# First layer's table products and chunk scan of the S5 branch: issued on GpSimd instead of VectorE

## The chip, the cores and the metric

The kernel runs on one core of a Trainium2 chip. The metric is the device time of one execution in microseconds (us), given as the median of several runs. TensorE (PE), VectorE (DVE), ScalarE (ACT), GpSimd (POOL) and SyncE (SP, which issues all the DMAs here) each work through a list of instructions of their own, in the order of that list; semaphores tie the lists together.

## What is computed

The reference runs two layers of a hybrid diffusion backbone over 128 context tokens and 512 latent tokens with a model width of 1024, in float32. Each layer forms a modulated input, one large projection of it, three branches, a gated merge and an MLP. The branch that matters here is the bidirectional S5 recurrence:

```
step = exp(log_step);  lam_bar = exp(lam * step)
b_bar = ((lam_bar - 1) / lam) * b
for d, rev in ((0, False), (1, True)):
    bu = einsum('blgc,gpc->blgp', u, b_bar[d])          # (+ lam_bar * s0 at the first token)
    states = scan(x[t] = lam_bar[d] * x[t-1] + bu[t])   # complex, 32 groups x 64 states
    y += einsum('blgp,gcp->blgc', states, c[d]).real
    finals.append(last state)
y = gelu(y + d_skip * u);  y = y * sigmoid(y @ w_glu)
```

The other two branches are a windowed and a global attention with 8 query heads each; the new keys, values and final S5 states are outputs too.

## The kernel before

**Chunks.** The kernel cuts the tokens into chunks of 8 and lays them out in 84 columns (context 0 to 17, latent 18 to 83, with one spare column for an initial state at either end). Within a chunk the recurrence is a matrix: one operator takes 8 inputs to the state contribution of the chunk (built in `s5_prep`), one takes the state ahead of a chunk to its 8 outputs (`ct`, built in `s5_tables`), and one takes the chunk's inputs to its outputs (`KK`, later `mg`, also from `s5_tables`). What is left is a recurrence over the chunk columns, which `s5_states` runs in the tile `st` [128 partitions, 84 columns, 2 (re, im), 32 groups].

**Tables.** `s5_tables` makes eight pieces b of four groups each. For every piece it forms `ct` from the input `Cm` and the powers `ec` with six products, sums and differences of 128x512 elements, through its helper `tt` (line 467): two into `mm`, one into half of `ct`, twice over. `ct` goes to DRAM by a DMA of SP (line 484). GpSimd clears `Bs` (line 487), ACT fills it (488 to 490), and TensorE multiplies `Cm` and `ct` with `Bs` (lines 496 and 498) into a bank `p_pt`, which DVE and ACT empty into `KK` (501, 502). `mm`, `ct` and `Bs` have one buffer each, so a piece can overwrite `ct` only when the matmuls and the DMA of the piece before have read it. In the first layer the pieces are drawn out of the generator during the windowed attention; in the second layer they were made during the MLP of the first.

**Scan.** `s5_states` first folds pairs of columns (`pairs(2, 3)`, four blocks of columns on DVE, lines 685 and 686), then walks 31 steps of two columns with four dependent operations each (lines 702 to 705: two products with the squared operator `M`, two sums); the first eight steps carry context and latent together (128x128 elements), the other 23 the latent alone (128x64). `pairs(1, 2)` then fills the columns in between, again in four blocks: the first block reads states up to column 19, the last one the very last state. After that `fin` is taken (line 709) and the backward half is reversed (lines 712 to 716). Only then do the matmuls of line 1055 read `st` and the `ct` tables (as `tab`).

**Order.** A scheduler of the framework sets the order within each engine's list when the program is built, by its own simulated timeline. So attention, projections, tables and scan of the first layer stand mingled in each list. While the windowed attention of layer 0 runs, DVE has to subtract for every weight tile (line 127, `wlo<-raw,whi`), empty and rotate projections (742 to 744), take row maxima of the scores (951), and so on. GpSimd has little to do: it clears tiles and takes three kinds of powers (lines 270, 776, 817); DVE's line 777 waits for the power of line 776.

Of the kernel before, what the change touches and what calls it, by code (L numbers as in the profile page):

```python
# [9 lines left out]
ALU = mybir.AluOpType  # L10
# [21 lines left out]
def net(tc, I, O, depth=DEPTH, dbg=None):  # L32
    nc = tc.nc
    V, S, G, T, SY = nc.vector, nc.scalar, nc.gpsimd, nc.tensor, nc.sync
    dbg = dbg or {}

    def ap(t, off, dims):
        return bass.AP(tensor=t.tensor, offset=t.offset + off, ap=[list(d) for d in dims])
# [4 lines left out]
    def dump(name, t):  # L43
        if name in dbg:
            SY.dma_start(dbg[name], t)
# [20 lines left out]
    def ppt():  # L66
        return bank("pt", 2)
# [391 lines left out]
    def s5_tables(l, pl_, keep):  # L459

        Bb, ec, dP, delta, vw, ew = (keep[n] for n in ("Bb", "ec", "dP", "delta", "vw", "ew"))

        def pt(name, shape, bufs=1):
            return pl_.tile(shape, F32, name=name, tag=f"{name}_{l}", bufs=bufs)

        def tt(o, a, b, op):
            V.tensor_tensor(o, a, b, op=op)

        for b in range(8):
            gs = slice(4 * b, 4 * b + 4)  # L470
            s4 = slice(0, 4)
            Cm = pt("Cm", [128, 2, 4, 16], 2)
            SY.dma_start(Cm, I["ssm_c"][l, :, :, gs])
            S.activation(Cm[:, 1], Cm[:, 1], AF.Copy, scale=-1.0)
            mm, ct = (pt(n, [128, 2, 4, 8, 16]) for n in ("mm", "ct"))
            m1, m2 = mm[:, 0], mm[:, 1]

            tt(m1, vw(Cm, 0, s4), ew(ec, 0, gs), ALU.mult)
            tt(m2, vw(Cm, 1, s4), ew(ec, 1, gs), ALU.mult)
            tt(ct[:, 0], m1, m2, ALU.add)  # L480
            tt(m1, vw(Cm, 1, s4), ew(ec, 0, gs), ALU.mult)
            tt(m2, vw(Cm, 0, s4), ew(ec, 1, gs), ALU.mult)
            tt(ct[:, 1], m1, m2, ALU.subtract)
            SY.dma_start(ctab_d[l][b], ct)

            Bs = pt("Bs", [128, 2, 4, 48])
            G.memset(Bs, 0.0)
            S.activation(Bs[:, :, :, 0:16], Bb[:, :, gs], AF.Copy)
            S.activation(Bs[0:64, :, :, 16:32], Bb[0:64, :, gs], AF.Copy)
            S.activation(Bs[64:128, :, :, 32:48], Bb[64:128, :, gs], AF.Copy)  # L490
            yield
            p = ppt()
            for q in range(4):
                o = p[32 * q:32 * q + 32]
                for r_ in range(2):
                    T.matmul(o[:, 0:16], Bs[:, r_, q, 0:32], Cm[:, r_, q, :], start=(r_ == 0), stop=(r_ == 1))
                for r_ in range(2):
                    T.matmul(o[:, 16:144], Bs[:, r_, q, 16:48], ct[:, r_, q].rearrange("p t o -> p (t o)"), start=(r_ == 0), stop=(r_ == 1))
            if b % 4 == 0:
                KK = pt("KK", [128, 4, 144])  # L500
            V.scalar_tensor_tensor(KK[:, b % 4, 0:16], delta, dP[:, b:b + 1], p[:, 0:16], op0=ALU.mult, op1=ALU.add)
            S.activation(KK[:, b % 4, 16:144], p[:, 16:144], AF.Copy)
            if b % 4 == 3:

                g0 = 4 * (b - 3)
                for q in range(4):
                    o = (g0 + q) * 3840
                    SY.dma_start(ap(kk_d[l], o + 7 * 16, [[240, 16], [4 * 3840, 4], [1, 128]]), KK[32 * q:32 * q + 16, :, 0:128])
                    SY.dma_start(ap(kk_d[l], o, [[240, 16], [4 * 3840, 4], [1, 112]]), KK[32 * q + 16:32 * q + 32, :, 32:144])
                for j in range(8):  # L510
                    SY.dma_start(mg_d[l][16 * j:16 * j + 16, g0:g0 + 16], ap(kk_d[l], g0 * 3840 + (7 - j) * 16, [[240, 16], [3840, 16], [1, 128]]))
            yield


    def phase_a(l, h):
# [94 lines left out]
        def ubuf():  # L610
            return sp.tile([128, 704], F32, name="ub", tag="ub", bufs=2)

        def s5_in(b, io):

            if b % 2 == 0:
                ubs[0] = load_u(b // 2)
            ub = ubs[0]
            for r_ in range(2):
                p = psc()
                for q in range(4):  # L620
                    T.matmul(p[:, q * NCH:(q + 1) * NCH], io[:, r_, q], ub[:, (b % 2) * 4 + q], start=True, stop=True)
                v = p[:, :4 * NCH].rearrange("p (g c) -> p c g", g=4)
                S.activation(st[0:64, 1:NCH, r_, 4 * b:4 * b + 4], v[0:64, 0:NCH - 1], AF.Copy)
                for a, e in segs:
                    S.activation(st[64:128, a + 1:e, r_, 4 * b:4 * b + 4], v[64:128, e - 1:a:-1], AF.Copy)
# [32 lines left out]
        def s5_states():  # L658

            for b in range(8) if l > 0 else ():  # L660
                io = sp.tile([128, 2, 4, 128], F32, name="tab", tag="tab", bufs=TAB)
                SY.dma_start(io, inop_d[l][b])
                s5_in(b, io)
            G.memset(st[:, 0:2], 0.0)
            G.memset(st[64:128, 18], 0.0)


            L0, L1 = lam8[l][:, 0], lam8[l][:, 1]
            M = sp.tile([128, 4, 2, 32], F32, name="l16")
            V.tensor_copy(M[:, 2, 0], L0[:, 0])  # L670
            V.tensor_copy(M[:, 2, 1], L1[:, 1])
            V.tensor_tensor(M[:, 3], L1, M[:, 2, ::-1], op=ALU.mult)
            V.tensor_tensor(M[:, 2], L0, M[:, 2], op=ALU.mult)
            V.tensor_tensor(M[:, 2], M[:, 2], M[:, 3], op=ALU.add)
            V.tensor_copy(M[:, 0], M[:, 2, 0:1].to_broadcast([128, 2, 32]))
            V.tensor_scalar(M[:, 1, 0], M[:, 2, 1], -1.0, None, op0=ALU.mult)
            V.tensor_copy(M[:, 1, 1], M[:, 2, 1])

            def pairs(src, dst):

                for e, k, n in ((V, 0, 10), (V, 10, 10), (V, 20, 10), (V, 30, 11)):
                    x_, o = (st[:, c + 2 * k:c + 2 * (k + n) - 1:2] for c in (src, dst))
                    tm = ubuf()[:, 0:64 * n].rearrange("p (n a b) -> p n a b", a=2, b=32)
                    for xv, lv in ((x_, L0), (x_[:, :, ::-1], L1)):
                        e.tensor_tensor(tm, xv, lv.unsqueeze(1).to_broadcast([128, n, 2, 32]), op=ALU.mult)
                        e.tensor_tensor(o, o, tm, op=ALU.add)

            pairs(2, 3)
            SY.dma_start(st[:, 19], I["state0"][:, l])
            for s in range(31):  # L690
                a = sp.tile([128, 2, 2, 32], F32, name="sa", tag="sa", bufs=1)
                c = sp.tile([128, 2, 2, 32], F32, name="sb", tag="sb", bufs=1)
                ns = 2 if s < 8 else 1
                cur = 2 * s + (1 if ns == 2 else 19)

                def at(i):
                    return st[:, i:i + 1] if ns == 1 else st[:, i:i + 19:18]

                def lb(t):
                    return t.unsqueeze(1).to_broadcast([128, ns, 2, 32])  # L700

                V.tensor_tensor(a[:, 0:ns], at(cur), lb(M[:, 0]), op=ALU.mult)
                V.tensor_tensor(c[:, 0:ns], at(cur)[:, :, ::-1, :], lb(M[:, 1]), op=ALU.mult)
                V.tensor_tensor(a[:, 0:ns], a[:, 0:ns], at(cur + 2), op=ALU.add)
                V.tensor_tensor(at(cur + 2), a[:, 0:ns], c[:, 0:ns], op=ALU.add)
            pairs(1, 2)

            fin = sp.tile([128, 2, 2, 32], F32, name="fin", tag="sa", bufs=1)[:, 0].rearrange("p a b -> p (a b)")
            S.activation(fin, st[:, 17].rearrange("p a b -> p (a b)"), AF.Copy)

            for a, e, n in ((0, 18, 9), (18, 84, 10), (28, 74, 10), (38, 64, 10), (48, 54, 3)):
                x0, x1 = st[64:128, a:a + n], st[64:128, e - n:e]
                tm = ubuf()[64:128, 0:n * 64].rearrange("p (n a b) -> p n a b", n=n, a=2)
                S.activation(tm, x0, AF.Copy)
                V.tensor_copy(x0, x1[:, ::-1])
                S.activation(x1, tm[:, ::-1], AF.Copy)
            dump("st", st)
            return fin

        if l > 0:  # L720
            fin = s5_states()
# [131 lines left out]
        if l == 0:  # L853
            fin = s5_states()
# [185 lines left out]
        for b in range(8):  # L1040
# [9 lines left out]
            for q in range(4):  # L1050
                o = p[:, q * NCH:(q + 1) * NCH]
# [496 lines left out]
    for l in range(depth):  # L1548
        M = phase_a(l, h)
# [99 lines left out]
```

## Time and profile before

| quantity | value |
|---|---|
| median of 3 runs | 2345.88 us (2345.13 to 2347.99) |
| the profiled execution, own time | 2344.87 us |
| its span in the trace | 2343.1 us |
| PE busy | 2252.5 us (96% of the span) |
| DVE busy | 1570.4 us (67%) |
| ACT busy | 1083.2 us (46%) |
| POOL busy | 40.5 us (2%) |

Busy shares are means over the whole program. Stretches of the span are told by their start and end in us from the span's start. In the rows below, `a<-b` names the tile written and the tiles read; "idle before" is what the engine sat idle just ahead of an instruction, with the one that ended the wait. TensorE's granted clock is given as a share of full speed.

### The profile page before, as it was taken

The page shows a single profiled execution, that of the slowest core. Times are in us where ns is not written, and L with a number is a line of the kernel's source. Part 1 is how long each engine was busy: PE and PEld are TensorE (multiplying, and loading weights), DVE is VectorE, ACT ScalarE, POOL GpSimd, SP SyncE. Part 2 cuts the span into 40 slices and gives each one's busy share as a digit, 9 for nine tenths or more (in the row PEclk, how much of TensorE's full clock was granted, in tenths as well). Part 3 has the DMA queues.
Part 4 walks back from the last instruction along what each step waited for, and adds up shares of the span by engine and source line. Part 5 has one row for each costly group of instructions (what it writes and reads, how often), then busy time and mean ns, then how long its engine had stood idle before and what let it go on. Part 6 is the DMA issues. An engine that isn't in the chain of part 4 may idle for free. (4 is left out here: it accounts for less than half of the span.)

```text
span 2343.1 us, 38503 instructions
## 1 busy us (share of the span) xinstructions
PE 2252.5 (96%) x14736; PEld 2039.5 (87%) x14736; DVE 1570.4 (67%) x3471; ACT 1083.2 (46%) x2569; POOL 40.5 (2%) x75
## 2 busy tenths in 40 slices
PE   7998999999998999999999999989999989999998
PEld 4988896799997988887888998989999878999986
DVE  7789945766358955455667499357763596776688
ACT  3455554665344443222234457456652356444441
POOL 0000100000000000000000001000000000000000
PEclk9999999999999999999999999989999999999999
DMA  7423366622242345445454522552212412222231
GB/s 274 113 89 101 113 201 207 209 73 78 73 153 66 100 170 172 136 160 167 141 152 141 156 68 88 159 175 84 83 55 81 171 46 90 76 79 83 83 106 63
DMA packets 124536, 283.16 MB, mean 121 GB/s; under 512 B 37024, under 2 KB 56608, under 8 KB 124352
## 3 DMA queue, kind: packets, MB, share of 16 engines
q1 hardware_dynamic: 124352, 280.70, 37.6%
q8 instruction: 116, 1.90, 0.3%
q14 instruction: 68, 0.56, 0.1%
HBM read 243.59 MB, written 41.25 MB: 122 GB/s over the span
## 5 line engine op out<-in xcount | busy, mean ns | idle before, releaser
L126 ACT ACTIVATE whi<-raw 128x512 fp32r<-128x512 f32 x454 | 282.6, 631 | 409.4 <-PE p_g L1250 100.3
L127 DVE TENSOR_TENSOR wlo<-raw,whi 128x512 fp32r<-128x512 f32 x454 | 311.2, 690 | 228.8 <-ACT whi L126 220.8
L163 PE MATMUL p_g<-hl,whi 128*128 128x384 f32 (+1 forms) x1040 | 325.9, 314 | 5.9 <-DVE hl L127 5.9
L162 PE MATMUL p_g<-hh,whi 128*128 128x384 f32 (+1 forms) x1040 | 327.7, 316 | 0.3 <-DVE rt L743 0.3
L164 PE MATMUL p_g<-hh,wlo 128*128 128x384 f32 (+1 forms) x1040 | 325.8, 314 | 0.2
L163 PEld LDWEIGHTS p_g<-hl,whi 128*128 128x128 f32 x1040 | 199.9, 192 | 6.8 <-DVE hl L127 6.8
L162 PEld LDWEIGHTS p_g<-hh,whi 128*128 128x128 f32 x1040 | 199.6, 192 | 6.0 <-ACT rl L1422 4.2
L164 PEld LDWEIGHTS p_g<-hh,wlo 128*128 128x128 f32 x1040 | 199.3, 192 | 1.0 <-DVE wlo L127 0.9
L162 PE MATMUL p_g<-act,whi 128*128 128x384 f32 x448 | 141.8, 317 | 5.6 <-DVE mt L1120 3.4
L127 DVE TENSOR_TENSOR pl<-p_pt,ph 128x512 fp32r<-128x512 f32 (+1 forms) x176 | 103.3, 592 | 59.5 <-ACT ph L126 43.6
L163 PE MATMUL p_g<-act,whi 128*128 128x384 f32 x448 | 139.6, 312 | 0.0
L173 PE MATMUL p_g<-whi,hh 128*128 128x256 f32 x480 | 138.2, 290 | 1.2 <-DVE rt L743 0.7
L164 PE MATMUL p_g<-act,wlo 128*128 128x384 f32 x448 | 139.3, 311 | 0.0
L174 PE MATMUL p_g<-wlo,hh 128*128 128x256 f32 x480 | 137.3, 288 | 1.1 <-DVE wlo L127 1.1
L175 PE MATMUL p_g<-whi,hl 128*128 128x256 f32 x480 | 136.3, 286 | 0.0
L126 ACT ACTIVATE ph<-p_pt 128x512 fp32r<-128x512 f32 (+1 forms) x176 | 90.2, 522 | 78.4 <-PE p_pt L972 77.6
L163 PE MATMUL p_sc<-hl,whi 128*128 128x384 f32 (+1 forms) x384 | 120.0, 313 | 2.7 <-DVE hl L127 2.7
L162 PE MATMUL p_sc<-hh,whi 128*128 128x384 f32 (+1 forms) x384 | 120.8, 316 | 0.0
L164 PE MATMUL p_sc<-hh,wlo 128*128 128x256 f32 (+1 forms) x384 | 119.8, 312 | 0.0
L951 DVE TENSOR_REDUCE part<-p_sc 128x1 f32<-128x384 f32 (+2 forms) x160 | 83.4, 527 | 30.9 <-PE p_sc L941 19.4
L972 PE MATMUL p_pt<-ident,P 128*128 128x128 f32 x576 | 96.2, 278 | 7.7 <-ACT P L963 5.6
L1248 PE MATMUL p_sc<-whi,ff 128*128 128x512 f32 x248 | 98.9, 400 | 0.0
(538 smaller groups left out, 5957.4 us busy)
## 6 DMA issues: line engine op xcount, KB each, us to landing
raw<-in_w_mod_dram SPq DMA_DIRECT2D x96, 512.0 KB, 4.6
raw<-in_w_up_dram SPq DMA_DIRECT2D x64, 512.0 KB, 3.7
raw<-in_w_down_dram SPq DMA_DIRECT2D x64, 512.0 KB, 3.6
raw<-in_w_gate_dram SPq DMA_DIRECT2D x48, 512.0 KB, 3.6
raw<-in_w_br_dram SPq DMA_DIRECT2D x24, 512.0 KB, 7.4
raw<-in_w_q_dram SPq DMA_DIRECT2D x16, 512.0 KB, 3.7
ctab_d<-ct SPq DMA_DIRECT2D x16, 512.0 KB, 2.6
tab<-ctab_d SPq DMA_DIRECT2D x16, 512.0 KB
```

The lines of the kernel that those rows point to most:

```text
L126: S.activation(hi, src, AF.Copy)
L127: V.tensor_tensor(lo, src, hi, op=ALU.subtract)
L162: T.matmul(out, wh, tok(ah, t0, t1), start=(first and k == 0), stop=False)
L163: T.matmul(out, wh, tok(al, t0, t1), start=False, stop=False)
L164: T.matmul(out, wl, tok(ah, t0, t1), start=False, stop=(last and k == n - 1))
L173: T.matmul(out, ah, wh, start=(first and k == 0), stop=False)
L174: T.matmul(out, ah, wl, start=False, stop=False)
L175: T.matmul(out, al, wh, start=False, stop=(last and k == n - 1))
L951: V.reduce_max(part[:, 0, z_:z_ + 1], pp[z_][:, 0:n4], axis=AX.X, negate=True)
L972: T.transpose(p[:, (2 * (z - z0) + z_) * 128:(2 * (z - z0) + z_ + 1) * 128], Ps[z_][:, z * 128:(z + 1) * 128], ident)
L1248: T.matmul(banks[t], a_, wh, start=(k == 0), stop=False)
```

## The change

In layer 0 (`l == 0`) the helper `tt` of `s5_tables` and the four operations of each scan step are issued on GpSimd (`G`) instead of DVE (`V`). Layer 1 keeps DVE for both. The two foldings `pairs`, the making of `M`, the copies and everything else stay where they were.

```
 def tt(o, a, b, op):
-    V.tensor_tensor(o, a, b, op=op)
+    (V if l else G).tensor_tensor(o, a, b, op=op)
...
-    V.tensor_tensor(a[:, 0:ns], at(cur), lb(M[:, 0]), op=ALU.mult)
-    V.tensor_tensor(c[:, 0:ns], at(cur)[:, :, ::-1, :], lb(M[:, 1]), op=ALU.mult)
-    V.tensor_tensor(a[:, 0:ns], a[:, 0:ns], at(cur + 2), op=ALU.add)
-    V.tensor_tensor(at(cur + 2), a[:, 0:ns], c[:, 0:ns], op=ALU.add)
+    (V if l else G).tensor_tensor(a[:, 0:ns], at(cur), lb(M[:, 0]), op=ALU.mult)
+    (V if l else G).tensor_tensor(c[:, 0:ns], at(cur)[:, :, ::-1, :], lb(M[:, 1]), op=ALU.mult)
+    (V if l else G).tensor_tensor(a[:, 0:ns], a[:, 0:ns], at(cur + 2), op=ALU.add)
+    (V if l else G).tensor_tensor(at(cur + 2), a[:, 0:ns], c[:, 0:ns], op=ALU.add)
```

Since the scheduler orders the whole program anew, all lists differ for the first 400 us or so, and in places of layer 1. In the pieces below a number after a tile's name tells its buffers apart (`ct_2371` is the `ct` of table piece 3, `mm_2625` and `Bs_2634` belong to piece 4, `p_pt_2639` is the bank of piece 4).

GpSimd's list from the clearing of `st` on, before: clearings and one power, nothing else.

```order
L664 MEMSET st_717 128x128 [waits Activation_49,Pool_49]
L487 MEMSET Bs_2180 128x384 [waits PE_49]
L487 MEMSET Bs_2343 128x384 [waits PE_49,Activation_49,Pool_49]
L776 ISA
L776 TENSOR_TENSOR ksq_1642<-ksq_1642,mh_73 128x10 [waits DVE_49]
L487 MEMSET Bs_2379 128x384 [waits PE_49,Activation_49,Pool_49]
L487 MEMSET Bs_2634 128x384 [waits PE_49,Activation_49,Pool_49]
```

GpSimd's list after the change, at table piece 3, in the middle of the scan's steps with one state column (128x64):

```order
L467 TENSOR_TENSOR ct_2371<-mm_2370 128x512 [waits DMAHW2_49,PE_49]
L487 MEMSET Bs_2379 128x384
L705 TENSOR_TENSOR st_717<-sa_1936,sb_1937 128x64 [waits Pool_49]
L467 TENSOR_TENSOR mm_2370<-Cm_2367,ec_0_305 128x512 [waits Pool_49]
L467 TENSOR_TENSOR mm_2370<-Cm_2367,ec_0_305 128x512
L702 TENSOR_TENSOR sa_1942<-st_717,l16_1804 128x64 [waits Pool_49]
L703 TENSOR_TENSOR sb_1943<-st_717,l16_1804 128x64
L467 TENSOR_TENSOR ct_2371<-mm_2370 128x512 [waits Pool_49]
L704 TENSOR_TENSOR sa_1942<-sa_1942,st_717 128x64 [waits Pool_49]
L467 TENSOR_TENSOR mm_2625<-Cm_2622,ec_0_305 128x512 [waits DMAHW6_49,Pool_49]
L467 TENSOR_TENSOR mm_2625<-Cm_2622,ec_0_305 128x512 [waits Activation_49]
L705 TENSOR_TENSOR st_717<-sa_1942,sb_1943 128x64 [waits Pool_49]
```

So scan and tables now share one list, and a table operation that waits for TensorE (`PE_49`) or for a DMA holds the scan behind it. In that list, from the first operation of the scan to its last, stand 32 scan operations of 128x128, 92 of 128x64, 24 table operations of 128x512, four clearings of `Bs` and the power of line 776.

DVE's list at the end of the scan, before: the last operations of the scan, and behind them the last block of `pairs(1, 2)` (`ub_2035`, line 685) with no wait for another engine; this stands far behind table piece 4.

```order
L704 TENSOR_TENSOR sa_2014<-sa_2014,st_717 128x64 [waits DVE_49]
L705 TENSOR_TENSOR st_717<-sa_2014,sb_2015 128x64 [waits DVE_49]
L685 TENSOR_TENSOR ub_2035<-st_717,lam8_100 128x704 [waits DVE_49]
L715 COPY st_717<-st_717 64x576 [waits Activation_49]
L686 TENSOR_TENSOR st_717<-st_717,ub_2035 128x11x64 [waits DVE_49]
L987 TENSOR_TENSOR qw_1128<-p_pv_2794,yt_2887 64x256 [waits PE_49,Activation_49]
L988 TENSOR_TENSOR qw_1128<-p_pv_2794,yt_2887 64x256
L951 TENSOR_REDUCE part_3094<-p_sc_3096 128x1 [waits PE_49]
L951 TENSOR_REDUCE part_3136<-p_sc_3137 128x1 [waits PE_49]
L897 SCALAR_TENSOR_TENSOR qs_2904<-p_pt_2905,qs_2904 64x4x128 [waits Activation_49]
L898 SCALAR_TENSOR_TENSOR qs_2904<-p_pt_2905,qs_2904 64x4x128
L685 TENSOR_TENSOR ub_2035<-st_717,lam8_100 128x704 [waits DVE_49]
```

DVE's list after the change, at the same block: it now stands just ahead of the query tile `qs_2612` and of the score maxima of the third block of queries, and ahead of the matmuls of table piece 4.

```order
L987 TENSOR_TENSOR qw_1128<-p_pv_2510,yt_2595 64x256 [waits PE_49,Activation_49]
L988 TENSOR_TENSOR qw_1128<-p_pv_2510,yt_2595 64x256
L685 TENSOR_TENSOR ub_2035<-st_717,lam8_100 128x704 [waits Pool_49]
L1002 TENSOR_TENSOR qw_1128<-qw_1128,p_pt_2606 128x512 [waits DVE_49]
L897 SCALAR_TENSOR_TENSOR qs_2612<-p_pt_2613,qs_2612 64x4x128 [waits PE_49,Activation_49]
L898 SCALAR_TENSOR_TENSOR qs_2612<-p_pt_2613,qs_2612 64x4x128
L951 TENSOR_REDUCE part_2795<-p_sc_2797 128x1 [waits PE_49]
L742 TENSOR_TENSOR rt_3747<-p_g_3717,rq_1118 128x256 [waits DMAHW4_49,Activation_49]
L686 TENSOR_TENSOR st_717<-st_717,ub_2035 128x11x64 [waits DVE_49]
L743 TENSOR_TENSOR rt_3747<-p_g_3717,rq_1118 128x256
L951 TENSOR_REDUCE part_2841<-p_sc_2842 128x1 [waits PE_49]
L715 COPY st_717<-st_717 64x576 [waits Activation_49]
```

What moved: the 172 operations are gone from DVE's list, the blocks of `pairs(1, 2)` stand earlier among the attention's work, and the first operation of each of the four blocks now carries a wait for GpSimd.

## Rows read from the trace of the kernel before

**Rows 1.** Busy time, share and instructions by engine, from the page.

```profile
PE 2252.5 (96%) x14736; PEld 2039.5 (87%) x14736; DVE 1570.4 (67%) x3471; ACT 1083.2 (46%) x2569; POOL 40.5 (2%) x75
```

**Rows 2.** Stretches: length, busy PE, PEld, DVE, ACT, POOL, granted clock, DMA.

```profile
140.00:240.00 100.00, 89.93 (x794) 82.95 (x790) 92.48 (x247) 54.95 (x217) 4.16 (x5) 0.95 0.32 100
240.00:300.00 60.00, 55.23 (x448) 49.86 (x440) 54.43 (x137) 36.78 (x96) 8.52 (x4) 0.97 0.42 132
...
170.00:180.00 10.00, 6.16 (x35) 4.78 (x33) 9.92 (x28) 3.14 (x12) 0.55 (x1) 0.79 0.37 139
180.00:190.00 10.00, 8.87 (x57) 8.63 (x58) 9.63 (x37) 6.49 (x31) 0.00 (x0) 0.69 0.09 29
...
1340.00:1460.00 120.00, 115.46 (x905) 109.45 (x904) 113.21 (x324) 75.57 (x260) 9.26 (x2) 0.99 0.26 77
```

**Rows 3.** PE's waits, 140 to 310: in all, times, longest (us).

```profile
PE p_pt L972 <- ACT P L963: 2.7, 3, 1.3
PE p_pt L496 <- POOL Bs L487: 2.4, 2, 1.2
PE p_pt L496 <- DVE qs L898: 2.2, 2, 1.4
PE p_pv L980 <- DVE pl L127: 2.1, 3, 1.0
```

**Rows 4.** DVE by line and shape, 140 to 300: count, busy us, mean ns.

```profile
L467 DVE TENSOR_TENSOR mm<-Cm,ec 128x512 f32<-128x512 f32 x26 | 16.8, 690 | 0.0
L467 DVE TENSOR_TENSOR ct<-mm 128x512 f32<-128x512 f32 x14 | 9.6, 688 | 0.0
L702 DVE TENSOR_TENSOR sa<-st,l 128x64 f32<-128x64 f32 x23 | 5.1, 223 | 0.3
L702 DVE TENSOR_TENSOR sa<-st,l 128x128 f32<-128x128 f32 x8 | 2.3, 291 | 0.0
```

**Rows 5.** DVE in order of time: where the scan can start, where it ends.

```profile
143.45 0.83 DVE L686 TENSOR_TENSOR st<-st,ub 128x640 f32<-128x640 f32 x1
...
278.22 0.23 DVE L705 TENSOR_TENSOR st<-sa,sb 128x64 f32<-128x64 f32 x1
278.48 0.89 DVE L685 TENSOR_TENSOR ub<-st,lam 128x704 f32<-128x704 f32 x1
```

**Rows 6.** GpSimd by line and shape, whole span: count, busy us, mean ns, idle.

```profile
L817 POOL TENSOR_TENSOR ssq<-ssq,mh 128x40 f32<-128x40 f32 x2 | 14.5, 7261 | 73.9 <-DVE ssq L815 73.9
L487 POOL MEMSET Bs<- 128x384 f32 x16 | 6.7, 418 | 927.3 <-PE p_pt L498 506.7 <-PE p_g L163 395.3 <-ACT P L963 25.1
L664 POOL MEMSET st<- 128x128 f32 x2 | 0.4, 210 | 109.7 <-ACT st L625 109.7
```

**Rows 7.** GpSimd in order of time: the powers of lines 776 and 817, one of line 270.

```profile
168.07 2.48 POOL L776 TENSOR_TENSOR ksq<-ksq,mh 128x10 f32<-128x10 f32 x1 [1.70 <-DVE ksq L775]
...
248.19 7.26 POOL L817 TENSOR_TENSOR ssq<-ssq,mh 128x40 f32<-128x40 f32 x1 [7.06 <-DVE ssq L815]
...
726.26 0.54 POOL L270 TENSOR_TENSOR ve<-mv,mh 128x1 f32<-128x1 f32 x1 [4.46 <-DVE ve L269]
...
1376.85 2.00 POOL L776 TENSOR_TENSOR ksq<-ksq,mh 128x10 f32<-128x10 f32 x1 [57.02 <-DVE ksq L775]
```

**Rows 8.** PE in order of time: the matmuls of table piece 4 start.

```profile
239.38 0.27 PE L496 MATMUL p_pt<-Cm,Bs 128*32 128x16 f32 x4 [0.78 <-DVE qs L898]
```

**Rows 9.** DVE in order of time, while GpSimd works on line 817's power.

```profile
250.19 0.68 DVE L467 TENSOR_TENSOR ct<-mm 128x512 f32<-128x512 f32 x1
...
251.06 0.82 DVE L686 TENSOR_TENSOR st<-st,ub 128x640 f32<-128x640 f32 x1
```

**Rows 10.** DVE by line and shape, 144 to 240: largest groups with two SBUF inputs.

```profile
L127 DVE TENSOR_TENSOR wlo<-raw,whi 128x512 fp32r<-128x512 f32 x14 | 9.7, 691 | 1.6 <-ACT whi L126 1.6
L686 DVE TENSOR_TENSOR st<-st,ub 128x640 f32<-128x640 f32 x7 | 5.8, 824 | 0.0
...
L685 DVE TENSOR_TENSOR ub<-st,lam 128x640 f32<-128x640 f32 x6 | 4.9, 824 | 0.0
...
L744 DVE TENSOR_TENSOR rt<-rt 128x256 f32<-128x256 f32 x6 | 2.5, 424 | 0.0
```

## The prediction, made before the changed kernel was run

> **What bounds the kernel now.** I read the busy shares first: TensorE is busy 96% of the span [rows 1], so only what makes TensorE wait, or slows its clock, can move the time. Next the stretches of layer 0 in which the moved work lies [rows 2]. From 140 to 240 DVE is busy 92.5 of 100 us and TensorE 89.9: TensorE idles 10.1 us there, and the mean granted clock is 0.95. From 240 to 300 DVE is busy 54.4 of 60 and TensorE idles 4.8, at 0.97. The clock falls at one place: TensorE idles 3.8 us between 170 and 180, and the granted clock is 0.79 there and 0.69 in the next 10 us, a mix of its two levels, 2.4 and 1.2 GHz. The same stage of layer 1, where the scan runs on DVE but no tables are made, has DVE just as full (113 of 120 us) and still leaves TensorE only 4.5 us idle, 3.8%, at a clock of 0.99 [rows 2]. So a full DVE alone does not starve TensorE; short waits on what DVE delivers late do: maxima that ScalarE's exponentials wait for, the low parts `pl`, the queries `qs` [rows 3]. That is the ground on which the change can gain or lose.
>
> **What leaves DVE.** In 140 to 300 the 40 table operations take 16.8 + 9.6 = 26.4 us, the 124 scan operations 4 x 5.1 + 4 x 2.3 = 29.6 us [rows 4] (lines 703 to 705 are like line 702 to 0.01 us each); eight more table operations of about 0.69 us, 5.5 us, lie ahead of 140. So DVE loses 56 of its 147 us in that stage. If nothing were late in return, TensorE's idle time in 140 to 240 could fall to layer 1's 3.8% (from 10.1 to 3.8) and the clock's loss from 5 us to 1: 10.3 us gained. In 240 to 300 the same gives 4.8 - 2.3 + 60 x 0.02 = 3.7 us.
>
> **What comes onto GpSimd.** No row shows GpSimd multiplying or adding tiles, so its price has to be bounded. Below stands clearing a tile, which only writes: 418 ns for 384 columns, 210 for 128 [rows 6], so 0.81 ns per column. Above stands the power, a two-input operation that takes 7.26 us for 40 columns [rows 6], far dearer per column; what is of use there is its fixed part. Widths 10 (the undisturbed 2.00 us) and 40 give [rows 6, 7] 0.175 us per column and 0.25 us fixed; widths 1 and 10 (0.54 and 2.00 us) give 0.38 fixed. I take 0.31 us fixed, the middle, and per column three times that, rounded up to 2.46 ns, since an operation here reads two streams and writes one. That makes 0.47 us for 64 columns, 0.63 for 128, 1.57 for 512, against 0.22, 0.29 and 0.69 on DVE.
>
> **The chain that this makes.** The scan cannot start before the first two blocks of `pairs(2, 3)` are done, at 143.45 + 0.83 = 144.3 [rows 5]; this is set by the S5 input matmuls and stays. In GpSimd's new list 32 operations of 128 columns, 92 of 64, 24 of 512, four clearings and one power stand from the scan's first operation to its last: 148 x 0.31 + 22,272 columns x 2.46 ns = 45.9 + 54.8, plus 4 x 0.42 + 2.5 for clearings and power, 104.9 us. The scan so ends at 249.2 if GpSimd never waits for anyone. That is earlier than before (278.4, rows 5), but DVE's list was rearranged for it: the last block of `pairs(1, 2)` now stands in front of the third query tile, and its wait for GpSimd holds everything behind it in DVE's list, the `wlo` subtractions, `qs`, the maxima and the emptying of projections. TensorE's matmuls of table piece 4 stand behind that `qs`; before, they began at 239.4 [rows 8], and then too they had waited for it. So DVE, then ScalarE and TensorE, wait for GpSimd until 249.2 where they were at 239.4: **9.8 us later**. The gain of 10.3 us in the same stretch is not to be had beside it, for there TensorE would run ahead only to wait. The three other blocks make the same kind of wait on the way and are part of this one.
>
> **The rest.** Behind that point the gain of 3.7 us stands against the table pieces 5 and 7, which are made hand to hand with the piece before: from the last matmul of the even piece to the last of the odd piece's operations GpSimd does four operations and a clearing, 4 x 1.57 + 0.42 = 6.7 us, where DVE took 4 x 0.69 and the clearing lay beside it, 3.2 us with it in line. TensorE already waited 1.2 us at two such places, the waits on `Bs` [rows 3]. The excess is 2 x 3.5 = 7 us with no other work for TensorE and 0 with enough; I take half, 3.5. That leaves -0.2. Nothing is charged for SP, whose eight stores of `ct` now wait for GpSimd with weight loads behind them: they are late by the same wait, which is counted. Nor for the power of line 817, which stands behind the scan's end, as before. The first eight table operations, now 12.6 us on GpSimd from about 55 on, end long before TensorE's first table matmuls at about 152. Layer 1 and the MLPs keep their work; their reordered lists count as zero.
>
> **Sum.** 2344.87 + 9.8 - 0.2 = 2354.5 in the profiled execution. Its time is 1.0 below the median of the runs, so 2355.5; I say 2355. A measurement of this kernel can tell about 0.2%, 4.7 us, from no change; +9.6 is 0.4%.
>
> **Rival 1, faster.** GpSimd's fixed part is the deciding number. TensorE's stretch to table piece 4 leaves the chain 239.4 - 144.3 = 95.1 us; with the columns' 54.8 and the 4.2 for clearings and power, the fixed part breaks even at 36.1 / 148 = 0.24 us, just below the lower end of my estimate, 0.25. If it is nearer 0.1, as for the smallest clearings, the chain is 74 us, GpSimd keeps ahead, and the gain is 10.3 + 3.7 - 3.5 = 10.5: 2334.4, or 2335 as a median. For it: the fixed part of the power may belong to the power's own routine. Against it: most steps of the scan wait for the operation just before. The Trainium skill (GPSIMD Engine Reference, section 3.1, Elementwise — side-by-side cycle accounting) gives 4497 ns for a GpSimd addition of 2048 columns; scaled by columns, an estimate from that page, the chain would be 53 us and this rival would hold. No row here shows such an operation.
>
> **Rival 2, much slower: the two engines hinder one another.** DVE's remaining work between 144 and 240 includes operations with both inputs in SBUF, in its four largest groups 9.7 + 5.8 + 4.9 + 2.5 = 22.9 us [rows 10]. If these and GpSimd's cannot run at once, the chain is 104.9 + 22.9 = 127.8 and ends at 272: +33 us, 2377. It decides as soon as more than a third of that time collides. Against it: while GpSimd worked 7.26 us on line 817, DVE's `ct<-mm` and `st<-st,ub`, both with two SBUF inputs, took 0.68 and 0.82 us, their usual times [rows 9, 4, 10]. But that power reads only 40 columns in 7 us; a multiplication reads all the time. The Trainium skill (SBUF — State Buffer, section Who interferes with whom) says that a DVE instruction with two SBUF inputs and a GpSimd instruction that reads SBUF contend, and that whoever starts first holds the shared ports for the whole instruction. By that rule this rival holds; the rows on the power speak against the "whole instruction".
>
> **Rival 3, no change.** With a fixed part of 0.25 the chain is 96 us, GpSimd arrives with TensorE, and what DVE gains is eaten by the handovers: 2346, within 4.7 us either way. That the operations stay on DVE after all is ruled out by the order.
>
> **Numbers.** Forecast (2351 to 2366): 0.36. Rival 2 (2366 to 2380): 0.14. Rival 3 (2341 to 2351): 0.20. Rival 1 (2330 to 2341): 0.30. So faster 0.30, within 0.2% 0.20, slower 0.50. Eight in ten: I leave out the upper part of rival 2 and the lowest of rival 1: 2335 to 2370. The forecast's own range is 2351 to 2366.
>
> **What would show it.** Lines 702 to 705 on GpSimd near 0.47 and 0.63 us and line 467 near 1.57; the scan's last operation at about 249; DVE's first line 685 of the last block idle until then, with `Pool` as its releaser; table piece 4's matmuls near 249 instead of 239; DVE some 60 us less busy. It is wrong, on the fast side, if those operations take 0.3 us and 1.2 us and DVE never waits for GpSimd; wrong on the slow side if DVE's `wlo` subtractions, 0.69 us now, stretch while GpSimd works.

## The result, and the profile of the changed kernel

The changed kernel takes 2361.9 us (median; 2358.3 to 2362.5), the kernel before 2345.6 beside it. The ratio is 1.0063, with a 95% interval from 1.0051 to 1.0075: slower by 0.6%, about 15 us. The profiled execution took 2362.5 us, its span is 2360.4.

The page's busy times by engine, to be held against [rows 1]:

```profile
PE 2258.8 (96%) x14736; PEld 2050.0 (87%) x14736; DVE 1550.7 (66%) x3299; ACT 1083.9 (46%) x2569; POOL 161.7 (7%) x247
```

DVE gave away 172 operations with durations of 61.5 us in all (56.0 from [rows 4] and the 5.5 ahead of 140), and is only 1570.4 - 1550.7 = 19.7 us less busy. Not all of the difference is lengthened work. Neighbours in DVE's list overlap by 0.08 us or a little more (before, a step of the scan starts at 240.36 and lasts 0.22 us, and the next operation starts at 240.49), so the 172 took up some 61.5 - 172 x 0.08 = 48 us, an estimate. Set against the median of their group before, 50 of the operations that stayed are longer by over 0.1 us each, 26 us in all, all of them in the first 400 us. GpSimd gained 161.7 - 40.5 = 121 us.

Stretches of the changed kernel, columns as in [rows 2]; the last is layer 1's scan, which here lies some 19 us later:

```profile
60.00:100.00 40.00, 32.30 (x234) 32.06 (x234) 25.70 (x46) 15.91 (x45) 6.20 (x6) 0.87 0.51 127
140.00:240.00 100.00, 85.71 (x709) 79.69 (x708) 76.94 (x135) 47.08 (x180) 84.83 (x126) 0.90 0.31 95
240.00:300.00 60.00, 52.26 (x396) 49.15 (x396) 42.31 (x73) 36.30 (x110) 32.86 (x44) 0.91 0.32 100
1360.00:1480.00 120.00, 115.12 (x898) 109.14 (x895) 112.52 (x324) 74.52 (x259) 9.26 (x2) 0.99 0.26 79
```

The first of these stretches before:

```profile
60.00:100.00 40.00, 39.65 (x299) 38.88 (x300) 26.50 (x54) 20.76 (x60) 0.15 (x1) 0.96 0.46 128
```

TensorE is busy for 85.7 of 100 us from 140 to 240 (89.9 before) and for 52.3 of 60 behind it (55.2 before), at a granted clock of 0.90 and 0.91 instead of 0.95 and 0.97, while DVE has fallen from 92 to 77%. And there is a loss where none was expected: between 60 and 100 TensorE is busy for 32.3 of 40 us, before for 39.7. Layer 1 is as it was.

The early stretch in three views: TensorE's wait (40 to 100), then VectorE and GpSimd in order of time, the first column the start, the second the duration:

```profile
PE p_pt L575 <- ACT hf L580: 7.7, 1, 7.7
```

```profile
57.29 1.78 DVE L127 TENSOR_TENSOR wlo<-raw,whi 128x512 fp32r<-128x512 f32 x1
58.98 0.15 DVE L555 TENSOR_TENSOR modc<-p_pv,bmodT 128x8 f32<-128x8 f32 x1
59.06 3.02 DVE L296 TENSOR_TENSOR prow<-Bb,ei 128x512 f32<-128x512 f32 x2
62.00 3.25 DVE L127 TENSOR_TENSOR wlo<-raw,whi 128x512 fp32r<-128x512 f32 x2
65.18 1.06 DVE L557 TENSOR_SCALAR affA<-modc 128x4 f32<-128x4 f32 x1
...
66.22 0.68 DVE L127 TENSOR_TENSOR wlo<-raw,whi 128x512 fp32r<-128x512 f32 x1
```

```profile
58.59 2.94 POOL L467 TENSOR_TENSOR mm<-Cm,ec 128x512 f32<-128x512 f32 x2
61.61 1.59 POOL L467 TENSOR_TENSOR ct<-mm 128x512 f32<-128x512 f32 x1
63.28 2.93 POOL L467 TENSOR_TENSOR mm<-Cm,ec 128x512 f32<-128x512 f32 x2
```

While GpSimd makes the first table products, a `wlo` takes 1.6 to 1.8 us, and 0.68 as soon as GpSimd has done (66.22). `affA`, four columns, takes 1.06. `modc`, which reads PSUM, keeps its 0.15. The next `hf` of line 580 needs `affA` and `affB`; ScalarE waits 7.8 us for them and TensorE 7.7. Before, ScalarE waited 3.8 us there and TensorE 3.0 us in three pieces, and `affA` was short:

```profile
60.47 0.17 DVE L557 TENSOR_SCALAR affA<-modc 128x4 f32<-128x4 f32 x1
```

GpSimd by line and shape from 140 to 310, then in order of time where VectorE left it alone, and the scan's end with what stands behind it on VectorE and TensorE:

```profile
L467 POOL TENSOR_TENSOR mm<-Cm,ec 128x512 f32<-128x512 f32 x24 | 30.9, 1307 | 0.2
...
L702 POOL TENSOR_TENSOR sa<-st,l 128x64 f32<-128x64 f32 x23 | 11.6, 505 | 1.6
...
L702 POOL TENSOR_TENSOR sa<-st,l 128x128 f32<-128x128 f32 x8 | 7.8, 973 | 10.7 <-DMA st<-in_state_dram 10.4
```

```profile
170.50 2.15 POOL L467 TENSOR_TENSOR mm<-Cm,ec 128x512 f32<-128x512 f32 x2
172.62 0.45 POOL L702 TENSOR_TENSOR sa<-st,l 128x128 f32<-128x128 f32 x1
...
174.68 0.45 POOL L704 TENSOR_TENSOR sa<-sa,st 128x128 f32<-128x128 f32 x1
```

```profile
249.37 0.32 POOL L705 TENSOR_TENSOR st<-sa,sb 128x64 f32<-128x64 f32 x1
```

```profile
249.79 0.89 DVE L685 TENSOR_TENSOR ub<-st,lam 128x704 f32<-128x704 f32 x1
```

```profile
252.20 0.30 PE L496 MATMUL p_pt<-Cm,Bs 128*32 128x16 f32 x4
```

Undisturbed, an operation takes 0.32 us for 64 columns, 0.45 for 128, 1.07 for 512 (the row of two says 2.15; the `ct` ones 1.26 to 1.29). That is about 0.19 us and 2.0 ns per column.

### The profile page after: what moved, and what is told of

Read it like the earlier page. It is cut to its first block, busy times and chain, and to the rows that moved or that the text cites. A ratio compares the mean times of both kernels' runs of the same rounds, so it can differ in the third digit from the quotient of the medians.

```text
span 2360.4 us, 38505 instructions
## 1 busy us (share of the span) xinstructions
PE 2258.8 (96%) x14736; PEld 2050.0 (87%) x14736; DVE 1550.7 (66%) x3299; ACT 1083.9 (46%) x2569; POOL 161.7 (7%) x247
## 4 chain that ended last, share of the span: by engine, by line
PE 81%; DVE 8%; DMA 4%; POOL 3%; ACT 2%; issue 1%; SPq 1%; DVEq 0%; ACTq 0%; POOLq 0%
PE p_g L162 8%; PE p_g L163 8%; PE p_g L164 8%; PE p_sc L1248 3%; PE p_sc L1250 3%; PE p_sc L1249 3%; PE p_sc L162 2%; PE p_sc L164 2%; PE p_sc L163 2%; PE p_g L1248 2%; PE p_g L1250 2%; PE p_g L1249 2%; PE p_pt L972 2%; PE p_g L173 2%; PE p_g L174 2%; PE p_g L175 2%
## 5 line engine op out<-in xcount | busy, mean ns | idle before, releaser
L127 DVE TENSOR_TENSOR wlo<-raw,whi 128x512 fp32r<-128x512 f32 x454 | 319.3, 708 | 245.3 <-ACT whi L126 236.6
L162 PEld LDWEIGHTS p_g<-hh,whi 128*128 128x128 f32 x1040 | 201.7, 194 | 13.7 <-ACT st L716 5.4
L173 PEld LDWEIGHTS p_g<-whi,hh 128*128 128x128 f32 x480 | 94.0, 196 | 7.3 <-issue 4.2
```

The source lines that it names most:

```text
L127: V.tensor_tensor(lo, src, hi, op=ALU.subtract)
L162: T.matmul(out, wh, tok(ah, t0, t1), start=(first and k == 0), stop=False)
L173: T.matmul(out, ah, wh, start=(first and k == 0), stop=False)
```

## The experiments

Three theories are weighed. **T**, turns: VectorE and GpSimd cannot both work on operands in SBUF, so each waits for the other's instruction. **C**, the chain, the forecast's own: only GpSimd's slower operations and the waits on their results count. **W**, which the first runs forced: VectorE waits in its own list, at line 685, for a scan that GpSimd finishes late. Each ratio is to the kernel before beside it. The table gives the delay against the kernel before in the profiled executions, from the starts of the first attention matmul (line 940, before at 152.2), of the first matmul of line 1055 (298.2), of the first power of line 270 (720.7) and from the spans. It is one execution each; the input's transfers alone scatter it by up to 3 us.

| kernel | ratio (95%) | 940 | 1055 | 270 | span |
|---|---|---|---|---|---|
| changed | 1.0063 (1.0051 to 1.0075) | 7.7 | 14.8 | 19.5 | 17.3 |
| scan only | 1.0081 (1.0064 to 1.0098) | 2.5 | 20.6 | 18.1 | 16.5 |
| tables only | 1.0015 (1.0004 to 1.0026) | 12.4 | 16.4 | 10.2 | 6.3 |
| early tables back | 1.0006 (0.9998 to 1.0015) | -0.5 | 2.5 | 1.4 | -0.4 |
| early tables alone | 1.0019 (1.0010 to 1.0028) | 5.6 | 7.1 | 6.9 | 4.0 |
| scan and pairs | 0.9995 (0.9986 to 1.0003) | 2.7 | 7.4 | 2.1 | 0.4 |
| idle products | 1.0062 (1.0049 to 1.0074) | 2.9 | 18.0 | 15.5 | 14.2 |
| idle clearings | 1.0005 (0.9996 to 1.0014) | -0.6 | 0.0 | -1.8 | -4.1 |

The starts mark places in lists that are not the same from run to run. From line 1055 to line 270, where GpSimd has at most 3.5 us of the moved work left, the kernel before takes 422.5 us, the changed kernel 427.2, early tables back 421.4, scan and pairs 417.3 and tables only 416.3. One wait that can be seen there is TensorE's near 450, at line 200, for a sum of VectorE (`mtmp`, line 193); before, then in the changed kernel:

```profile
PE p_g L200 <- DVE mtmp L193: 5.0, 1, 5.0
```

```profile
PE p_g L200 <- DVE mtmp L193: 5.1, 2, 4.7
```

Tables only, early tables back, and scan and pairs wait at most 0.9 us at this line. So up to some 5 us of a ratio, either way, can come from the new order of the lists alone. The two idle runs of the table, whose lists are those of before, are free of this.

**The decisive pair: work that nobody reads.** The kernel before, with operations on two small tiles of their own added to GpSimd behind the initial state. The lists of TensorE, VectorE and ScalarE stay word for word as they were, so nothing but GpSimd's activity differs.

```diff
+    G.tensor_tensor(dm[:, 0:64], dm[:, 0:64], st[:, 19]..., op=ALU.mult)
+    for k_ in range(100):                 # idle products
+        G.tensor_tensor(*((dn, dm, dm) if k_ % 2 == 0 else (dm, dn, dn)), op=ALU.mult)
```

> The kernel before with 100 operations added on GpSimd that nobody reads: products of 128x128 tiles (0.45 us undisturbed in the changed kernel, 45 us in all), behind the initial state that the scan also waits for, so from about 146 us on. All other engines keep their lists word for word. Theory T: VectorE's operations with both operands in SBUF (`wlo`, lines 685, 686, 744, 467, 702 to 705) stretch while they run, `wlo` from 0.69 to about 0.9 us, 15 to 25 us in all; VectorE is 95% full there, so the kernel is 5 to 20 us above before. Theory W: nobody waits for these operations but three clearings of `Bs` behind them: within 3 us of before, no stretching.

For the other run the loop writes only:

```diff
+    for k_ in range(210):                 # idle clearings
+        G.memset(dm, 0.0)
```

> The same with 210 clearings of a 128x128 tile (0.21 us each, 44 us in all) in place of the 100 products: GpSimd is as long busy but reads nothing. Theory T, if it is the reading of SBUF that collides: no stretching, within 3 us of before. If any access of GpSimd collides: as with the products. Theory W: within 3 us of before.

Products: 2359.2 us, 1.0062. Clearings: 2346.4, 1.0005. VectorE by line and shape, 148 to 206, with products (line 710 is the scan's first operation, 702 before):

```profile
L467 DVE TENSOR_TENSOR mm<-Cm,ec 128x512 f32<-128x512 f32 x8 | 6.3, 831 | 0.0
L127 DVE TENSOR_TENSOR wlo<-raw,whi 128x512 fp32r<-128x512 f32 x8 | 5.9, 734 | 2.9 <-ACT whi L126 2.9
L710 DVE TENSOR_TENSOR sa<-st,l 128x128 f32<-128x128 f32 x8 | 3.2, 401 | 0.0
```

and with clearings:

```profile
L467 DVE TENSOR_TENSOR mm<-Cm,ec 128x512 f32<-128x512 f32 x11 | 7.1, 688 | 0.0
L127 DVE TENSOR_TENSOR wlo<-raw,whi 128x512 fp32r<-128x512 f32 x9 | 6.2, 688 | 1.6 <-ACT whi L126 1.6
...
L710 DVE TENSOR_TENSOR sa<-st,l 128x128 f32<-128x128 f32 x7 | 2.0, 288 | 0.0
```

TensorE's waits from 140 to 240, with products:

```profile
PE p_pt L496 <- DVE qs L906: 4.9, 1, 4.9
PE p_pv L988 <- DVE pl L127: 4.5, 2, 4.2
```

58 us of unread products cost as much as the whole change. T's collisions are shown: VectorE is 10.8 us longer busy by the pages (1581.2 against 1570.4), and TensorE waits longer for `qs` and `pl`. C alone, which has no collisions, falls. But not all of the price is turns, for GpSimd's own work stood behind the products too: the power of line 776, for which VectorE waited 2.3 us, and the clearings of `Bs`, for which ScalarE waited from 140 to 300

```profile
ACT Bs L488 <- POOL Bs L487: 13.2, 4, 7.9
```

in place of 2.8 us before and 4.6 with clearings. Since VectorE's list is the same as before, each operation can be set against itself: from 150 to 205 it falls 14.3 us further behind, 9.3 of them by longer operations and the other 5 by longer waits. Clearings (43 us) leave VectorE's times alone. The Trainium skill (SBUF — State Buffer, section Who interferes with whom) says that a VectorE instruction with two SBUF inputs contends with GpSimd instructions that read SBUF and not with those that only write; these two runs agree.

**One operand instead of two.** The same with copies:

```diff
+    for k_ in range(150):                 # idle copies
+        G.tensor_copy(*((dn, dm) if k_ % 2 == 0 else (dm, dn)))
```

> As the run with idle products, with 150 copies of a 128x128 tile on GpSimd, one operand read instead of two, near 0.25 us each, some 37 us in all; the other engines keep their lists but for one ScalarE instruction three places later. If every reading of SBUF by GpSimd takes turns with VectorE's two-operand work: `wlo` and the scan's operations stretch as with the products, 8 to 14 us above before. If only GpSimd's two-operand forms do: as with the clearings, within 3 us of before.

2347.2 us, 1.0011 (1.0003 to 1.0020), on the clearings' side of the expectation by time. By the trace the copies take turns too: undisturbed a copy takes 0.29 us, and its mean is

```profile
L697 POOL COPY dn<-dm 128x128 f32<-128x128 f32 x75 | 37.7, 503 | 4.3
```

and VectorE is 6.1 us longer busy (1576.5 on its page). The stretching is half that of the products, and the time hardly moved.

**Which half of the change costs.** Scan on GpSimd with tables on VectorE (the diff to the changed kernel), and the reverse, lines 702 to 705 on `V` again.

```diff
-            (V if l else G).tensor_tensor(o, a, b, op=op)
+            V.tensor_tensor(o, a, b, op=op)
```

> Layer 0's scan (lines 702 to 705) on GpSimd, its table products (line 467) on VectorE as before. Theory T, the two engines take turns wherever both read or write SBUF: the 7.4 us that the changed kernel lost before 100 us, while GpSimd made table products, are gone; the scan's 44 us on GpSimd still stretch VectorE's two-SBUF-operand operations, by 15 to 20 us in all, against 29.6 us taken off VectorE, and TensorE gets little of the rest: 2343 to 2352 us. Theory C, only GpSimd's own chain and the waits on it count: without the tables the chain is 92 x 0.32 + 32 x 0.45 = 44 us, ends near 200 instead of 250, nobody waits for it, and VectorE is 29.6 us freer: 2336 to 2342 us, with no stretched VectorE operation.

> Layer 0's table products on GpSimd, its scan on VectorE as before. Theory T: eight of the table operations again lie between 54 and 67 us, beside the affine coefficients of the second half of the input, so TensorE again waits about 7 us there; later tables cost another 0 to 5: 2351 to 2359 us. Theory C: the early operations end long before TensorE's first table matmuls at 152 and cost nothing; VectorE is 33 us freer, against 2 to 4 us of later handovers: 2341 to 2348 us.

Scan only: 2364.7 us, worse than T and C had it; VectorE's operations are 4.8 us longer, not T's 15 to 20, while the scan itself takes 71.5 us on GpSimd instead of C's 44. Tables only: 2348.0, at C's upper end and below T's range; the early loss is there (TensorE busy for 31.1 of 40 us from 60 to 100), and the run is still 16.4 us late at line 1055. Some 10 of these are made up behind, where hardly any of the moved work lies. For scan only, VectorE's wait from 140 to 300 and the stretch from 180 to 205:

```profile
DVE ub L685 <- POOL st L705: 12.4, 4, 5.1
```

```profile
180.00:205.00 25.00, 7.10 (x34) 5.50 (x33) 18.10 (x35) 6.46 (x38) 23.35 (x45) 0.63 0.13 45
```

Four times VectorE stood at line 685, 12.4 us in all, with `pl` and the maxima queued behind; TensorE worked for 7.1 of 25 us there and its clock was at 0.63, much of it at the lower of the two levels. That is W. It is the wait that the forecast had named, at other places.

**The cure for W.** Everything that reads the scan's result follows it to GpSimd.

```diff
+                        e = V if l or src == 2 else G
-                V.tensor_copy(x0, x1[:, ::-1])
+                (V if l else G).tensor_copy(x0, x1[:, ::-1])
```

> Scan alone on GpSimd as in the scan-only run, and with it everything of the states that reads the scan's result: the second `pairs` (lines 685 and 686, 16 operations of 640 or 704 columns, about 1.5 us each on GpSimd) and the copies of line 715. VectorE then has no operation left that waits for the scan. Theory W: the 12.4 us of VectorE's waits at line 685 in the scan-only run, and TensorE's two waits of 6 us that follow, are gone: 2338 to 2350 us, 14 us or more below the scan-only run; the states are needed only near 300 us. Theory T alone: GpSimd works 24 us more, 13 us of it collide; VectorE's stretching grows: 2360 to 2372 us.

2342.9 us, 0.9995: 22 us below scan only, although GpSimd works longer (131.5 against 103.0 us on the pages) and VectorE no less (1558.3 against 1556.5). At line 1055 the run is 7.4 us late instead of 20.6: 13 us regained, about as much as VectorE's waits at line 685. So W is shown as the main cause of that run's loss; the rest of the 22 us arises behind that line, in the other lists. It is no gain over the kernel before: TensorE still worked only 27.6 of 40 us between 180 and 220, and made it up behind.

**The early tables.** Taken out of the change (`piece[0]` is the number of the table piece), and then alone:

```diff
+            (V if l or piece[0] < 2 else G).tensor_tensor(o, a, b, op=op)     # back
+            (G if l == 0 and piece[0] < 2 else V).tensor_tensor(o, a, b, op=op)     # alone
```

> The changed kernel with table pieces 0 and 1 (12 of the 48 table operations) on VectorE again; pieces 2 to 7 and the scan stay on GpSimd. Theory T: TensorE's wait of 7.7 us near 60 us goes, the rest of the loss stays: 2352 to 2357 us, that is 5 to 9 us below the changed kernel. Theory C: those operations were never on the path, the chain after 144 us loses four operations of 1.3 us: 2355 to 2362 us.

> Only table pieces 0 and 1 of layer 0 (12 of the 48 table operations) on GpSimd, all else as before. Theory T (GpSimd and VectorE take turns at SBUF): the stall of the changed kernel near 60 us comes back alone: TensorE waits 7 to 8 us for the affine coefficients' users there, VectorE's `wlo` and `prow` operations there take 1.2 to 1.8 us instead of 0.69, and the kernel is 5 to 9 us above before. Theory W (VectorE waits in its own list for the scan on GpSimd): no scan on GpSimd, no loss: within 2 us of before.

Back: 2346.7 us, 15 below the changed kernel where T expected 5 to 9. Alone: 2348.9, 4.0 us above before (2.3 to 6.6 by the interval) at a wait of 7.7 us in the trace: T's sign, but below its 5 to 9. So the early stall is shown, with about 4 us. Where the rest of the 15 arose can be read from the table: the changed kernel is 8.2 us behind the run with the early tables back at the first attention matmul, 12.3 at line 1055 and 18.1 at line 270. The 4.1 before line 1055 (from 260 to 300 TensorE was busy for 40.0 of 40 us, in the changed kernel for 34.8) and the 5.8 behind it came with the rearranged lists and are not traced to one cause. One wait of C's kind is hardly the cause: ScalarE waits 13.7 us for the clearings of `Bs` in the run with the early tables back (11.0 in the changed kernel, 2.8 before), and that run is only 2.5 us late at line 1055.

**Halved operations.** The early tables alone, each operation cut into two of 256 columns:

```diff
+                for h_ in (0, 2):
+                    G.tensor_tensor(o[:, h_:h_ + 2], a[:, h_:h_ + 2], b[:, h_:h_ + 2], op=op)
```

> As the run with only table pieces 0 and 1 on GpSimd, each of their 12 operations cut into two halves of 256 columns (about 0.7 us instead of 1.1 to 1.3). Theory T, turns are taken instruction by instruction, so a short VectorE operation waits for the end of the GpSimd operation that is running, and its price is the length of that operation: TensorE's wait near 60 us falls from 7.7 to about 4 us, VectorE's `wlo` there from 1.6 to about 1.2 us; 1 to 4 us above before. If the collision only divides a rate between the two, the same total work costs the same: a wait of 7 to 9 us again and 4 to 6 us above before.

TensorE's wait (4.8 us near 60), and `wlo` and `affA`, near what T had:

```profile
PE p_pt L581 <- ACT hf L586: 5.4, 2, 4.8
```

```profile
56.73 1.13 DVE L127 TENSOR_TENSOR wlo<-raw,whi 128x512 fp32r<-128x512 f32 x1
...
62.16 0.60 DVE L563 TENSOR_SCALAR affA<-modc 128x4 f32<-128x4 f32 x1
```

The stall of one operation goes with the length of the GpSimd instruction beside it (about 1.46 us whole, 0.95 halved). The time did not follow: 2350.1 us, 1.0020 (1.0011 to 1.0029), 4.0 above before, where the two expectations meet, and no better than whole operations. The halves run on until 69 and stretch what comes there; VectorE's total is 1572.0 against 1572.6.

**Layer 1 instead of layer 0.** At all five places:

```diff
-(V if l else G).tensor_tensor(
+(G if l else V).tensor_tensor(
```

> The same move in layer 1 instead of layer 0: its tables (made between 970 and 1200 us, beside the first MLP, where VectorE is 55% busy) and its scan on GpSimd, layer 0 as before. Theory T: the tables' stretching meets slack and costs nothing; beside the scan VectorE is as full as in layer 0, gives 29.6 us and gets some 15 back, while TensorE idled only 4.5 us there: 2343 to 2351 us. Theory C: the chain of 44 us plus waits is shorter than the scan's time on a full VectorE, so a small gain: 2340 to 2346 us.

2352.2 us, 1.0035 (1.0022 to 1.0049): a loss, a little above T's range, not C's gain. The stretch of layer 1's tables, here and before, then VectorE's waits around layer 1's scan here:

```profile
900.00:1200.00 300.00, 300.00 (x1908) 251.69 (x1907) 153.25 (x257) 92.37 (x199) 53.67 (x47) 1.00 0.45 154
```

```profile
900.00:1200.00 300.00, 300.00 (x1908) 251.68 (x1907) 164.16 (x296) 92.62 (x198) 2.92 (x7) 1.00 0.46 154
```

```profile
DVE ub L685 <- POOL st L705: 10.6, 3, 5.2
...
DVE kf L777 <- POOL ksq L776: 6.1, 1, 6.1
```

(The first row is this run, the second the kernel before.) Beside the MLP, with VectorE half idle, 54 us of GpSimd work cost TensorE nothing. Beside the scan W came back, 10.6 us of it, and the power waited behind scan steps.

**Two versions meant to win.** The first joins two edits above, early tables back and the cure for W. The second gives GpSimd only scan steps 8 to 30, the copies and the second pairs, in eight short blocks:

```diff
+                (V if l or s < 8 else G).tensor_tensor(...)          # lines 702 to 705
-                for e, k, n in ((V, 0, 10), (V, 10, 10), (V, 20, 10), (V, 30, 11)):
+                cuts = (0, 10, 20, 30, 41) if l or src == 2 else (0, 5, 10, 15, 20, 25, 30, 35, 41)
```

> Both cures together: table pieces 0 and 1 on VectorE, pieces 2 to 7, the scan, the second `pairs` and the copies of line 715 on GpSimd. Neither the start nor VectorE's list then waits for the scan. Theory T and W together: GpSimd has about 122 us of its own work from 152 on and 25 to 35 us of turns with VectorE, so it ends near 300, just where the states are needed; VectorE is 45 us freer but stretched by as much as in the changed kernel: 2340 to 2350 us, no clear gain over before. If only the waits had cost (W): 2335 to 2341 us.

> A version meant to win: only what comes behind the first attention tiles goes to GpSimd, in short operations. Scan steps 0 to 7 and all tables stay on VectorE; steps 8 to 30 (64 columns, 0.32 us), the second `pairs` in eight blocks of 320 or 384 columns (about 0.8 us) and the copies of line 715 go to GpSimd. Theory T with W: GpSimd is idle until about 200, so the dense chain of maxima and rope operations between 180 and 200 is not touched; after it VectorE loses 35 us of work up to 278 and gets some 15 back: 2336 to 2345 us, 0 to 8 below before. If GpSimd's work costs VectorE as much as it takes off it wherever it stands: 2345 to 2352 us.

The first: 2354.9 us, 1.0042 (1.0030 to 1.0054), a miss. GpSimd, then VectorE, at one moment of it:

```profile
195.53 1.54 POOL L688 TENSOR_TENSOR ub<-st,lam 128x640 f32<-128x640 f32 x1
```

```profile
195.43 0.17 DVE L997 TENSOR_TENSOR stat<-stat 128x8 f32<-128x8 f32 x1
195.54 1.54 DVE L957 TENSOR_TENSOR stat<-part,nsink 128x2 f32<-128x2 f32 x1
```

A maximum over two columns, 0.16 us otherwise, started 10 ns behind a GpSimd operation and ended with it. The Trainium skill (SBUF — State Buffer, section Who interferes with whom) has whoever issues first hold the shared ports for the whole instruction. This row agrees. Long operations of GpSimd lie between 180 and 200, where maxima and rope products are short and each waits for the one before: from 181.6 to 190.8 two products of 640 and four of 256 columns (lines 780 to 787) took 8.9 us instead of 3.3, and TensorE waited 8.6 us for the `qw` behind them. The second version keeps clear of that place: 2344.4 us, 0.9993 (0.9984 to 1.0002), within the range of T with W. It ties with the kernel before; no version here is faster clear of noise.

## Why the prediction was right, and where it was not

**Direction and size** were right: 2361.9 lies in the forecast's own range, 2351 to 2366; +15 came instead of +9.6. That the number held is luck more than insight: the wait that made up the forecast's 9.8 us did not come about, and about 4 us of the loss, by the run with the early tables alone, arose at a place that it had put at nothing.

**GpSimd's price** was too high. Estimated were 0.47, 0.63 and 1.57 us, undisturbed are 0.32, 0.45 and 1.07 to 1.28. The fixed part, 0.19, lies below the 0.24 at which Rival 1 was to win. Its condition held, and it lost, because it left the turns out.

**The scan's end** was forecast at 249.2 and lies at 249.37 + 0.32 = 249.7: a hit by two errors that cancel. It began at 152.5 instead of 144.3: the kernel was late by then, and the first operation waited for the transfer of the initial state (line 689), which the forecast overlooked; it was issued at 150.7, before at 143.0. And it took 97 us instead of 105. At undisturbed prices the list is 92 x 0.32 + 32 x 0.45 + 16 x 1.07 + 8 x 1.28 + 4 x 0.42 + 2.0 = 75 us, and 22 us are longer operations, nearly all of them turns (about 2 are the scan's first operation, 2.64 us long; the first one behind that transfer is almost as long, 2.38 us, beside clearings): Rival 1's chain with Rival 2's collisions, put there at 22.9.

**VectorE's wait at the last block** did not happen in the changed kernel. Its waits for the scan come to 0.6 us; it reached the block only at 249.76, after a wait of 1.7 us for ScalarE. The mechanism is real: it cost 12.4 us where only the scan moved.

**Table piece 4** starts at 252.2 instead of 239.4 [rows 8], 12.8 us late where 9.8 were forecast. But 7.7 of them were there at the first attention matmul, 1.8 from a late start (line 553 at 54.26 instead of 52.47) and the rest from the step that failed: the first eight table operations were said to end long before TensorE's first table matmuls and to cost nothing. They did end in time. What they delayed was not their own reader but VectorE's other work, which stood on the path.

**VectorE's relief** was put at some 60 us and is 19.7. The sum of durations counted the overlaps of neighbours, and 26 us came back as longer operations. That ScalarE would stand behind GpSimd's clearings of `Bs`, 11.0 us instead of 2.8, was left out as well.

**The rest**, -0.2, was +4.5 (17.3 - 12.8): 6.7 us more up to 720, 2.2 regained behind. Kernels with other lists gain or lose as much there; this stays open.

**The point of the power** [rows 9] was read too kindly. It leaves VectorE alone for 7 us; the idle products did not (`sa` 401 ns instead of 291 [rows 4]), as the text itself had feared, and Rival 2 was given 0.14. Its victim was half right: the collisions did lengthen GpSimd's chain, but they hurt most where a short VectorE operation stands on TensorE's path.

## What to carry to other kernels

Products and sums on GpSimd are a second pair of hands only beside VectorE work with PSUM operands, or where VectorE has slack: of the 48 us that the moved operations took up on VectorE here, 26 came back as longer operations. Before moving work there, list the VectorE operations with operands in SBUF that will run beside it, and ask which of them TensorE waits for; each can be late by the length of one GpSimd instruction, however short it is. Look also at GpSimd's old work: its clearings and powers now stand behind the new. And move the readers with the producer, or the faster engine will stand in its list and wait for the slower one; that cured the scan-only run, though the version with both cures lost for another reason. Last, when the scheduler orders everything anew, look for waits far from the change before a few us are put down to it.

## What the runs showed of the hardware

- GpSimd's product or sum of two SBUF tiles costs about 0.19 us and 2.0 ns per column; its copy of 128 columns 0.29 us.
- Turns are taken by whole instructions, and not only products are caught: the four-column `affA` took 1.06 us beside 512-column products, 0.60 beside 256-column ones and 0.17 undisturbed, and a 64x512 copy (line 411) 1.24 us instead of 0.42 beside the first table product. GpSimd's power of 40 columns, 7.26 us, is the exception [rows 9]; why is not shown. VectorE operations that read PSUM keep their times (`modc` 0.15). Clearings by GpSimd cost VectorE nothing.
- Equal GpSimd time is not equal cost: 58 us of products cost 14 us (9.3 us of longer VectorE operations among them), 73 us of copies 2 to 3, 43 us of clearings nothing that could be measured.
